# Larger modulation runs, 96-row latent attention, and an issue order planned by other TensorE prices

## The chip, the cores and the metric

The kernel runs on one core of one Trainium2 chip. The metric is the device time of one execution in microseconds (us). A core has a matrix engine (TensorE, PE in the rows; its weight loads are PEld), a vector engine (DVE), a scalar engine (ACT), GpSimd (POOL), and a queue (SP) that issues the DMA transfers.

## The reference

Two networks one after the other, on 256 tokens of width 1024 and, in the first, 256 context tokens. Cut to what matters here:

```python
# first block, two layers: nine modulation vectors of 1024 for the tokens and nine for the context
mod_x = (jax.nn.silu(c) @ w_ada[l] + b_ada[l])[:, None, :]        # w_ada[l]: 1024 x 9216
mod_c = jax.nn.silu(c_ctx) @ w_ada[l] + b_ada[l]
h = h + 0.5 * g1 * _swiglu(_modulate(_rms_norm(h, norm_ffn1[l]), sh1, sc1), ...)
# then attention with windows, global and neighbourhood, and a second feed-forward net

# second block, one layer: a recurrent mixer in chunks (rwkv), latent attention (mla),
# differential attention, a gated merge, a feed-forward net with a convolution
q = (_rmsnorm(c_q, q_norm) @ w_uq).reshape(B, S, 8, 64 + 32)       # latent attention, 8 heads
q_rope = _apply_rope(q[..., 64:], cos, sin)                       # a part of 32 for each head
kv = (_rmsnorm(c_kv, kv_norm) @ w_ukv).reshape(B, S, 8, 64 + 64)
k_rope = _apply_rope(k_rope, cos, sin)                            # one part of 32 for all heads
logits = einsum(q_nope, k_nope) + einsum(q_rope, k_rope)          # over 64 and over 32
probs = _masked_softmax(logits * scale, mask)                     # causal
```

## The kernel before

The program is written once without an order: `Plan` records every operation with its engine, its operands and a cost from `Plan.cost`, and `Plan.schedule` then plays the engines forward in time. Whenever an engine is free in that play it takes the first ready operation in the order of writing whose buffers can be had. `emit` writes the instructions out in the order found, so each engine's order is fixed when the kernel is built. All come from one line of `emit` (L739 in the rows). Buffers are pages of SBUF (`page`), a small area (`small`), three slots for weights (`w`) and eight PSUM banks (`bank`).

Dense products split every f32 number into two f32r parts and take three f32r matmuls for each block (`mm3`). Other products stay in f32, and each of those stands as two passes in the trace.

The modulation vectors are made by `ada_steps`: for each layer five groups of up to 2048 columns, each in eight steps over the 1024 inputs. A step loads 1 MB of `w_ada` and issues four matmuls (two in the last group) that each use 32 columns of the array, so the four stand side by side. The steps are the filling (`fill`): one is popped after each block of a feed-forward net, which is where the planner then places its matmuls among the dense ones, one by one. The first group of the first layer runs in the setup.

Latent attention (`mla_diff`) keeps the 64-row parts of q and k in `qn` and `kn` (two heads in a tile, on 64 rows each) and the 32-row parts in `qr` and `kr` (on 32 rows each). The scores of one head and query tile are one matmul over 64 rows and one over 32 rows, added up in PSUM. A block of matmuls that uses part of the array has that shape as its "tile": the rows show it as rows*columns, 128*128 being the whole array.

`Run` puts several TensorE operations into one that the planner doesn't split.

Of the kernel before, what the change touches and what calls it, by code (L numbers as in the profile page):

```python
# [18 lines left out]
P = 128  # L19
# [368 lines left out]
class Plan:  # L388
# [20 lines left out]
    def record(self, eng, method, a, k):  # L409
        if self.open_run is not None:  # L410
            assert eng == "tensor"
            self.open_run.append((method, a, k))
            return None
        if method == "run":
            reads, writes, cost = [], [], 0.0
            for m_, a_, k_ in a:
                r_, w_ = self.operands(a_, k_)
                cost += self.cost(eng, m_, a_, k_, r_, w_)[0]
                reads += r_
                writes += w_  # L420
            return self.note(eng, method, a, {}, reads, writes, k["cost"] or cost, None)
# [50 lines left out]
    def cost(self, eng, method, a, k, reads, writes):  # L472
# [8 lines left out]
        src_ps = any(r.buf.kind == "ps" for r in reads)  # L481
        if eng == "tensor":
            if method == "transpose":
                return 110, None
            f32r = any(s[0] == "d" for s in reads[0].chain) or reads[0].buf.dt == F32R
            n = sh[1]
            for d in sh[2:]:
                n *= d
            if f32r and sh[0] == 32:
                return 75, None  # L490
            if f32r:
                return max(107, n / 2.4) + 1, None
            if sh[0] == 32 or o.index()[1] and sh[0] <= 64:
                return (0.52 * n if sh[0] == 32 else max(60, n / 0.95)), None
            return (max(109, n / 0.6) if sh[0] > 64 else max(107, n / 0.6)), None
        ns = [int(np.prod(r.shape[1:])) for r in reads]
# [17 lines left out]
    def schedule(self, n_pages, n_small, n_w, window, margin, n_banks=8):  # L514
# [44 lines left out]
        front, dma_free, t, n_done = 0, 0.0, 0.0, 0  # L559
        table, used = None, -1e9  # L560
        done = [False] * N
# [90 lines left out]
        while n_done < N:  # L652
            for e in engs:
                if busy[e] > t:
                    continue
                h, skipped, pick = ready[e], [], None
                while h and len(skipped) < 48:
                    i = heapq.heappop(h)
                    tab = ops[i][7]
                    if e == "scalar" and tab and tab != table and t - ready_at[i] < TABLE_WAIT and t - used < TABLE_WAIT:  # L660
                        heapq.heappush(events, (t + 300.0, 2, -1))
                        skipped.append(i)
                    elif can(i):
                        pick = i
                        break
                    else:
                        skipped.append(i)
                for i in skipped:
                    heapq.heappush(h, i)
                if pick is None:  # L670
                    continue
                cost, tab, lat = ops[pick][6:9]
                if e == "scalar" and tab:
                    if tab != table:
                        cost += 1283
                        table = tab
                    used = t + cost
# [63 lines left out]

TABLE_WAIT = 2500.0


class Build:
# [134 lines left out]
    def ada_steps(self, l, g):  # L880

        nc = self.nc
        n = min(2048, 9 * D - 2048 * g)
        nj = n // 512
        st = {}

        early = l == 0 and g == 0

        def load(k):
            def f():  # L890
                if k == 0:
                    st["ps"] = self.aux_ps("ada")
                raw = self.sb.tile([P, 2048], F32, name="araw", tag="araw0" if early else "araw",
                                   bufs=8 if early else 3)
                nc.sync.dma_start(raw[:, :n], self.a["w_ada"][l, k, :, 2048 * g:2048 * g + n])
                for j in range(nj):
                    nc.tensor.matmul(st["ps"][32 * j:32 * j + 32, :], self.cs[:, k, :],
                                     raw[:, 512 * j:512 * j + 512], start=(k == 0), stop=(k == KB - 1),
                                     skip_group_check=True, tile_position=(0, 32 * j))
            return f  # L900

        def fin():
            np_ = 32 * nj
            t = self.t("adat", [512])
            nc.vector.tensor_copy(t[:np_], st["ps"][:np_])
            pt = self.aux_ps("adaT")
            for b in range(4):
                nc.tensor.matmul(pt[:, 8 * b:8 * b + 8], t[:np_, 128 * b:128 * b + 128], self.rsel[:np_],
                                 start=True, stop=True)
            view = pt[:, :32].rearrange("p (b j r) -> p b j r", b=4, j=4)[:, :, :nj]  # L910
# [3 lines left out]
            for m in range(2 * g, 2 * g + nj // 2):  # L914
# [6 lines left out]
                elif m in (2, 8):  # L921
                    nc.vector.tensor_scalar(self.hg[l][m // 8], w, 0.5, None, op0=OP.mult)
        return [load(k) for k in range(KB)] + [fin]

# [950 lines left out]

    def rope32(self, dst, src):
# [6 lines left out]
        nc.vector.tensor_tensor(dst, t1, t2, op=OP.add)  # L1883

    def mla_diff(self, u):
# [31 lines left out]
        for i in range(3):  # L1917
# [5 lines left out]
            cn.append(c)  # L1923
        kr, qr = self.s2("kr", (S,)), self.s2("qr")
        self.rope32(kr, x[3])
        qn, kn = ([self.s2(f"{n}{i}") for i in range(2)] for n in ("qn", "kn"))
        w = self.wtile(a["w2_uq"])
        for i in range(3):
# [3 lines left out]
            if i < 2:  # L1932
                nc.scalar.copy(qn[i].rearrange("p a b -> p (a b)"), ps)
            else:
                t = self.t512("qrt")
                nc.scalar.copy(t, ps)
                for j in range(2):
                    self.rope32(qr[:, j], t[:, S * j:S * j + S])
        w = self.wtile(a["w2_ukv"])
        for i in range(2):  # L1940
            ps = self.mm_ps("pkn")
            for j in range(2):
                self.dense(ps[:, S * j:S * j + S], w, (2 * i + j) * P, cn[2:], nk=1)
            nc.scalar.copy(kn[i].rearrange("p a b -> p (a b)"), ps)
        vm = [self.s2(f"vm{i}", (512,)) for i in range(2)]
# [24 lines left out]
        def transposed(pr):  # L1970
            pt = self.aux_ps("PT2")
            for i in range(3):
                nc.tensor.transpose(pt[:, P * i:P * i + P], pr[:, P * i:P * i + P], self.ident)
            pts = self.t512("pts")
# [3 lines left out]
        for b in range(4):  # L1978
            yp = self.aux_ps("y")
            for s in range(2):  # L1980
                h = 2 * b + s
                hs = slice(64 * s, 64 * s + 64)
                rr = slice(32 * (h % 4), 32 * (h % 4) + 32)
                ps = self.aux_ps("Sml")
                for qt, (c0, c1) in enumerate(span):
                    qs = slice(P * qt, P * qt + P)
                    N = c1 - c0
                    nc.tensor.matmul(ps[:, c0:c1], qn[b // 2][hs, b % 2, qs], kn[b // 2][hs, b % 2, :N],
                                     start=True, stop=False)
                    nc.tensor.matmul(ps[:, c0:c1], qr[rr, h // 4, qs], kr[rr, :N], start=False, stop=True,  # L1990
                                     tile_position=(32 * (h % 4), 0))
                d = diag(ps[:, :3 * P])
# [4 lines left out]
                for i, (c0, c1) in enumerate(span):  # L1997
                    nc.vector.tensor_scalar(pr[:, c0:c1], pr[:, c0:c1], st[:, 4 + i:5 + i], None, op0=OP.mult)
                pts = transposed(pr)
                for qt in range(2):  # L2000
                    for kb in range(qt + 1):
                        c0 = (qt + kb) * P
                        nc.tensor.matmul(yp[hs, P * qt:P * qt + P], vm[kb][:, 64 * h:64 * h + 64], pts[:, c0:c0 + P],
                                         start=(kb == 0), stop=(kb == qt), skip_group_check=True)
            o = self.s2(f"oml{b}", (2, S), F32R)
# [78 lines left out]
def build(tc, aps, out):  # L2084
# [5 lines left out]
    b.second()  # L2090
    order = plan.schedule(N_PAGES, N_SMALL, W_SLOTS, 3000, dict(m=4096, s=64))
    with tc.tile_pool(name="sb", bufs=1) as sb, tc.tile_pool(name="ps", bufs=1, space=PSUM) as ps, tc.manual_schedule():
# [26 lines left out]
```

## Time and profile before

| | |
|---|---|
| median of 3 runs | 2465.49 us (2462.23 to 2465.62) |
| the profiled execution | 2465.52 us, of which the span of the trace is 2463.7 us |
| TensorE busy | 2419.1 us (98%), 14630 matmuls |
| VectorE, ScalarE, GpSimd busy | 1342.4 us (54%), 971.2 us (39%), 46.5 us (2%) |
| DMA | 133 GB/s on the mean |

The ends of matmuls are modelled in such a profile, and consecutive ones overlap, so 98% says that the matrix engine always has one in its pipe and not that it is at its peak. What one matmul costs is read from how many start in a stretch of known length. A row that counts matmuls in a stretch also counts the one to three whose tail reaches over its edges.

### The profile page before, as it was taken

What the parts mean: (1) busy time and instruction counts of PE and PEld (TensorE: products, weight loads), DVE (VectorE), ACT (ScalarE), POOL (GpSimd) and SP (SyncE); (2) the same over time, 40 slices, a digit from 0 to 9 for tenths busy, and PEclk for the clock granted to TensorE, in tenths of its full rate; (3) what the DMA queues carried; (4) which work ended last, traced back from release to release, by engine and by line L of the source; (5) the groups of instructions that cost most, each with busy time, mean ns of one, the idle gap of its engine ahead of it and who ended that gap; (6) DMA issues with size and microseconds to landing.
All of it is one profiled execution on the core that took longest, in us unless ns stands there. A gap on an engine that the chain in (4) does not pass through costs nothing. (4 is left out here: it accounts for less than half of the span.)

```text
span 2463.7 us, 35734 instructions
## 1 busy us (share of the span) xinstructions
PE 2419.1 (98%) x14630; PEld 2036.2 (83%) x14630; DVE 1342.4 (54%) x2533; ACT 971.2 (39%) x1748; POOL 46.5 (2%) x62
## 2 busy tenths in 40 slices
PE   7999999999999999999999999999999999999998
PEld 5777776978787677778878889889999897999998
DVE  4323332585753389335323347866567665657874
ACT  3222222476642122223212235755456122556653
POOL 0000000000000000000000000000000000000000
PEclk8999999999999999999999999999999997999999
DMA  7526523212234454343224223135554011354543
GB/s 312 205 103 240 197 87 127 95 44 87 85 137 161 146 190 180 131 156 139 91 71 137 75 100 103 61 113 178 196 171 164 22 52 35 104 190 169 190 168 123
DMA packets 55043, 328.35 MB, mean 133 GB/s; under 512 B 7134, under 2 KB 10206, under 8 KB 24799
## 3 DMA queue, kind: packets, MB, share of 16 engines
q1 hardware_dynamic: 54878, 326.07, 37.1%
q8 instruction: 114, 1.87, 0.3%
q14 instruction: 51, 0.41, 0.1%
HBM read 325.00 MB, written 1.05 MB: 132 GB/s over the span
## 5 line engine op out<-in xcount | busy, mean ns | idle before, releaser
L739 PE MATMUL bank<-page,page 128*128 128x256 f32 (+8 forms) x13152 | 2296.3, 346 | 29.0 <-DMA page<-in_w_ada_dram 13.2
L739 PEld LDWEIGHTS bank<-page,page 128*128 128x128 f32 (+3 forms) x13152 | 1876.1, 186 | 373.8 <-issue 95.1
L739 ACT CAST page<-w 128x1024 fp32r<-128x1024 f32 (+2 forms) x511 | 489.1, 961 | 1067.6 <-PE bank L739 1027.6
L739 DVE TENSOR_TENSOR page<-w,page 128x1024 fp32r<-128x1024 f32 (+2 forms) x511 | 567.8, 1113 | 591.5 <-ACT page L739 457.8
L739 DVE TENSOR_TENSOR page<-page,bank 128x512 f32<-128x512 f32 (+2 forms) x170 | 94.2, 570 | 245.3 <-PE bank L739 244.1
L739 PE MATMUL bank<-page 128*128 128x256 f32 (+5 forms) x650 | 167.0, 325 | 1.9 <-DVE page L739 1.3
L739 DVE SCALAR_TENSOR_TENSOR page<-bank,small,page 128x256 f32<-128x256 f32 (+2 forms) x240 | 111.5, 484 | 103.8 <-PE bank L739 100.2
L739 DVE TENSOR_TENSOR page<-page,page 128x256 fp32r<-128x256 f32 (+3 forms) x271 | 128.6, 490 | 12.1 <-ACT page L739 11.5
L739 ACT ACTIVATE page<-bank,small 128x256 f32<-128x256 f32 (+2 forms) x216 | 115.1, 546 | 37.3 <-DVE small L739 24.8
L739 PEld LDWEIGHTS bank<-page 128*128 128x128 f32 (+2 forms) x650 | 109.8, 188 | 15.9 <-issue 4.2
L739 ACT CAST page<-page 128x256 fp32r<-128x256 f32 (+1 forms) x167 | 78.2, 481 | 97.0 <-DVE page L739 86.5
L739 ACT COPY page<-bank 128x512 f32<-128x512 f32 (+2 forms) x163 | 77.6, 511 | 96.5 <-PE bank L739 91.1
L739 PEld LDWEIGHTS bank<-small,page 128*128 128x128 f32 (+1 forms) x760 | 93.2, 167 | 25.0 <-issue 8.7
L739 PE MATMUL bank<-small,page 128*128 128x128 f32 (+4 forms) x760 | 108.8, 269 | 4.1 <-ACT page L739 2.8
L739 ACT ACTIVATE page<-bank 128x512 f32<-128x512 f32 (+3 forms) x168 | 84.2, 508 | 61.3 <-PE bank L739 57.8
L739 ACT ACTIVATE page<-page 128x256 f32<-128x256 f32 (+3 forms) x180 | 78.0, 446 | 67.0 <-DVE page L739 60.0
L739 DVE TENSOR_TENSOR page<-bank,page 128x256 f32<-128x256 f32 (+2 forms) x123 | 57.5, 489 | 55.4 <-PE bank L739 29.6
L739 DVE TENSOR_REDUCE small<-bank 128x1 f32<-128x512 f32 (+3 forms) x132 | 67.5, 527 | 4.3 <-PE bank L739 4.0
L739 POOL TENSOR_TENSOR small<-small 128x2 f32<-128x2 f32 (+2 forms) x32 | 34.4, 1078 | 1874.3 <-DVE small L739 1382.8
L739 ACT ACTIVATE page<-page,small 128x256 fp32r<-128x256 f32 (+1 forms) x124 | 56.7, 507 | 30.5 <-DVE page L739 30.0
L739 DVE COPY_PREDICATED page<-page,small 128x384 f32<-128x384 uint32 x124 | 64.9, 590 | 1.0
L739 DVE TENSOR_SCALAR page<-page,small 128x256 f32<-128x256 f32 (+2 forms) x136 | 53.6, 408 | 2.2 <-ACT page L739 1.1
(46 smaller groups left out, 383.2 us busy)
## 6 DMA issues: line engine op xcount, KB each, us to landing
w<-in_gu_dram SPq DMA_DIRECT2D x88, 1024.0 KB, 5.0
page<-in_w_ada_dram SPq DMA_DIRECT2D x64, 1024.0 KB, 4.9
w<-in_dn_dram SPq DMA_DIRECT2D x64, 704.0 KB, 4.1
w<-in_w_up_dram SPq DMA_DIRECT2D x22, 1024.0 KB, 4.8
w<-in_w_qk_dram SPq DMA_DIRECT2D x12, 1024.0 KB, 4.8
w<-in_w_gate_dram SPq DMA_DIRECT2D x12, 1024.0 KB, 4.9
w<-in_w_dn_dram SPq DMA_DIRECT2D x16, 704.0 KB, 4.0
page<-in_w_ada_dram SPq DMA_DIRECT2D x16, 512.0 KB, 3.5
```

Source lines behind the costliest of these rows:

```text
L739: getattr(getattr(self.real, eng), m_)(*a_, **k_)
```

## The change

It has five parts. (1) In all groups of the modulation but the first, a step loads two pieces and issues their matmuls as one run that isn't split; in the last group of each layer (two matmuls for a piece) the two pieces go to different columns of the array. The loads have four buffers in place of three. (2) Latent attention copies both parts of q and k into tiles of 96 rows (`qh`, `kh`), with one matmul per head and query tile; ScalarE copies heads of 64 rows, VectorE writes the turned 32 rows head by head, GpSimd copies the shared `kr` to four heads at once, twice. (3) The two heads of a pair then share one run for the product with v. (4) `Plan.cost` has other prices for matmuls and gives each the shape that it uses, and `Plan.schedule` charges 100 ns for another shape and lets TensorE take a ready operation of the same shape ahead of one of another for up to 1.5 us. (5) The margin that stays free in SBUF when an operation is taken out of turn is 6144 in place of 4096.

```diff
             if method == "transpose":
-                return 110, None
-            f32r = any(s[0] == "d" for s in reads[0].chain) or reads[0].buf.dt == F32R
...
-            if f32r:
-                return max(107, n / 2.4) + 1, None
...
+                return 109, (128, 128, True)
+            mode = tuple(32 if x <= 32 else 64 if x <= 64 else 128 for x in (rows, cols)) + (False,)
+            if any(s[0] == "d" for s in reads[0].chain) or reads[0].buf.dt == F32R:
+                return max(107, n / 2.4) + 13.3, mode
+            return max(223 if mode[1] == 128 else 109, n / 0.6 + 8), mode
...
+                    if e == "tensor" and tab != shape and other is None and t - ready_at[i] < SHAPE_WAIT:
+
+                        other = i
+                        continue
...
+                if e == "tensor" and tab != shape:
+                    cost += 100
+                    shape = tab
...
-                for j in range(nj):
-                    nc.tensor.matmul(st["ps"][32 * j:32 * j + 32, :], self.cs[:, k, :],
...
+                with nc.run(cost=nk * nj * 215.0 + 200.0):
+                    for i, raw in enumerate(raws):
+                        k = k0 + i
+                        for j in range(nj):
+                            c = 32 * (j if nj == 4 else j + nj * i)
+                            nc.tensor.matmul(st["ps"][c:c + 32, :], self.cs[:, k, :], raw[:, 512 * j:512 * j + 512],
...
+        qh, kh = ([self.s2(f"{n}{i}", (4, S)) for i in range(2)] for n in ("qh", "kh"))
+        for i in range(2):
+            nc.gpsimd.tensor_copy(kh[i][64:96], kr[64:96, None, :].to_broadcast([32, 4, S]))
...
-                    nc.tensor.matmul(ps[:, c0:c1], qn[b // 2][hs, b % 2, qs], kn[b // 2][hs, b % 2, :N],
-                                     start=True, stop=False)
-                    nc.tensor.matmul(ps[:, c0:c1], qr[rr, h // 4, qs], kr[rr, :N], start=False, stop=True,
-                                     tile_position=(32 * (h % 4), 0))
+                    nc.tensor.matmul(ps[:, c0:c1], qh[h // 4][:96, h % 4, P * qt:P * qt + P],
+                                     kh[h // 4][:96, h % 4, :c1 - c0], start=True, stop=True)
...
+            with nc.run(cost=3 * 215.0):
                 for qt in range(2):
                     for kb in range(qt + 1):
...
-    order = plan.schedule(N_PAGES, N_SMALL, W_SLOTS, 3000, dict(m=4096, s=64))
+    order = plan.schedule(N_PAGES, N_SMALL, W_SLOTS, 3000, dict(m=6144, s=64))
```

Where the instructions stand now is read from the orders of the two programs. On TensorE, in the first layer's first feed-forward net, the modulation's matmuls (output 32x512, from `page_75`, which holds the silu of c) stood one at a time between the dense ones of a down projection:

```order
L739 MATMUL bank_70<-page_768,page_192 128x512
L739 MATMUL bank_71<-page_2122,page_75 32x512
L739 MATMUL bank_70<-page_199 128x512 x2
L739 MATMUL bank_70<-page_199,page_192 128x512
L739 MATMUL bank_70<-page_2014,page_199 128x512 x2
L739 MATMUL bank_70<-page_2014,page_192 128x512
L739 MATMUL bank_70<-page_2075,page_199 128x512 x2
L739 MATMUL bank_70<-page_2075,page_192 128x512
L739 MATMUL bank_70<-page_204,page_199 128x512 x2
L739 MATMUL bank_70<-page_204,page_192 128x512
L739 MATMUL bank_71<-page_2122,page_75 32x512
```

In the changed program eight of them stand together, four from each of two loads, again within a down projection:

```order
L747 MATMUL bank_68<-page_864,page_534 128x512 x2
L747 MATMUL bank_68<-page_864,page_225 128x512
L747 MATMUL bank_72<-page_396,page_239 128x512 x2
L747 MATMUL bank_74<-page_78,page_75 32x512 x4
L747 MATMUL bank_74<-page_961,page_75 32x512 x4
L747 MATMUL bank_72<-page_396,page_534 128x512
L747 MATMUL bank_72<-page_396,page_239 128x512 x2
```

Over the whole program the 288 modulation matmuls stood in 97 such groups: 3 of the setup, 32 of one matmul, 58 of two to four, 4 of five or six. Now they stand in 39: the same 3 of the setup, 28 of eight and 8 of four. Changes of shape on TensorE (transposes counted as a shape of their own) fell from 517 to 326.

On TensorE in the second block, the scores of latent attention: `page_10404` holds `qn` or `kn` (64 rows), `page_1431` `qr` (32 rows), the banks are the score tiles; a `small` input is the unit matrix of a transpose.

```order
L739 MATMUL bank_72<-page_10404,page_75 128x128
L739 MATMUL bank_72<-page_1431,page_13336 128x128
L739 MATMUL bank_72<-page_10404,page_75 128x256
L739 MATMUL bank_72<-page_1431,page_13336 128x256
L739 MATMUL bank_74<-page_10404,page_75 128x128
L739 MATMUL bank_74<-page_1431,page_13336 128x128
L739 MATMUL bank_74<-page_10404,page_75 128x256
L739 MATMUL bank_74<-page_1431,page_13336 128x256
L739 MATMUL bank_73<-small,page_3990 128x128
L739 MATMUL bank_70<-page_10404,page_13336 128x128
L739 MATMUL bank_73<-small,page_3990 128x128 x2
L739 MATMUL bank_70<-page_1431,page_13336 128x128
```

In the changed program `page_75` and `page_13377` are `kh`, `page_3927` and `page_4081` `qh`; `bank_73` takes a dense product.

```order
L747 MATMUL bank_73<-page_1873,page_5322 128x512
L747 MATMUL bank_70<-page_75,page_3927 128x128
L747 MATMUL bank_70<-page_75,page_3927 128x256
L747 MATMUL bank_67<-page_75,page_3927 128x128
L747 MATMUL bank_67<-page_75,page_3927 128x256
L747 MATMUL bank_69<-small,page_9752 128x128
L747 MATMUL bank_72<-small,page_9752 128x128
L747 MATMUL bank_71<-page_75,page_3927 128x128
L747 MATMUL bank_68<-page_75,page_3927 128x128
L747 MATMUL bank_68<-page_75,page_3927 128x256
L747 MATMUL bank_71<-page_75,page_3927 128x256
L747 MATMUL bank_73<-page_198,page_84 128x256
```

Thirty-two score matmuls over part of the rows became sixteen over the whole array, with dense ones between the heads. GpSimd, which ran five TENSOR_TENSOR in a row here, now has the two copies among them:

```order
L747 TENSOR_TENSOR small<-small 128x8
L747 TENSOR_TENSOR small<-small 128x4 x2
L747 COPY page_75<-page_9752 32x1024
L747 COPY page_13377<-page_9752 32x1024
L747 TENSOR_TENSOR small<-small 128x4
```

The first score matmul waits for the first copy, the fifth head's for the second; the 128x4 behind them belongs to the recurrent mixer's norm.

## Rows read from the trace of the kernel before

**Rows 1.** The page: span, engines, and TensorE's granted clock in 40 slices.
```profile
span 2463.7 us, 35734 instructions
PE 2419.1 (98%) x14630; PEld 2036.2 (83%) x14630; DVE 1342.4 (54%) x2533; ACT 971.2 (39%) x1748; POOL 46.5 (2%) x62
PEclk8999999999999999999999999999999997999999
```

**Rows 2.** The chain that ended last: start, length, engine, count of instructions.
```profile
1677.24 191.94 PE bank L739 x1599
2020.61 115.13 PE bank L739 x688
```

**Rows 3.** Whom TensorE waited for: us in total, times, longest.
```profile
PE bank L739 <- DMA page<-in_w_ada_dram: 13.2, 5, 6.6
PE bank L739 <- ACT page L739: 11.3, 19, 1.8
PE bank L739 <- DVE page L739: 10.0, 16, 2.3
PE bank L739 <- POOL small L739: 2.3, 5, 1.1
```

**Rows 4.** TensorE in chosen stretches: dense, six groups, eight singles, one and two ranks.
```profile
core 0: us, PE busy (x), PEclk, DMA share, GB/s
1320.00:1476.00 156.00, 156.00 (x690) 1.00 0.27 91
258.31:330.95 72.64, 72.64 (x339) 1.00 0.41 152
396.14:435.71 39.57, 39.57 (x150) 1.00 0.26 93
330.95:331.94 0.99, 0.99 (x10) 1.00 0.00 0
64.91:66.75 1.84, 1.84 (x14) 1.00 0.01 4
```

**Rows 5.** The latent scores' stretch: TensorE and its clock before and after 2062 us.
```profile
2055.18:2062.00 6.82, 6.82 (x42) 1.00 0.43 143
2062.00:2093.22 31.22, 31.22 (x81) 0.50 0.01 4
```

**Rows 6.** TensorE by shape, 2055.18 to 2093.22 us.
```profile
L739 PE MATMUL bank<-page,page 32*128 32x256 f32 x16 | 9.2, 673 | 0.0
L739 PE MATMUL bank<-page,page 64*128 64x256 f32 x16 | 8.7, 641 | 0.0
L739 PE MATMUL bank<-page,page 64*128 64x128 f32 x16 | 5.7, 454 | 0.0
L739 PE MATMUL bank<-page,page 32*128 32x128 f32 x16 | 5.7, 452 | 0.0
```

**Rows 7.** TensorE: 24 f32 passes of 128 columns, and 4 of 256.
```profile
2007.34:2009.93 2.59, 2.59 (x26) 1.00 0.27 111
1560.52:1561.39 0.87, 0.87 (x6) 1.00 0.88 367
```

**Rows 8.** All engines (PE, PEld, DVE, ACT, POOL) in the scores' stretch and behind it.
```profile
2055.18:2093.22 38.04, 38.04 (x121) 22.40 (x120) 15.24 (x54) 9.63 (x33) 1.05 (x1) 0.59 0.08 29
2093.22:2130.00 36.78, 36.78 (x266) 34.20 (x266) 14.88 (x30) 15.75 (x29) 0.00 (x0) 0.96 0.32 110
```

**Rows 9.** Groups on GpSimd, ScalarE and VectorE that are nearest to the added copies.
```profile
L739 POOL MEMSET page<- 64x512 f32 x20 | 10.4, 520 | 449.2 <-PE bank L739 448.5
L739 ACT COPY page<-bank 128x256 f32<-128x256 f32 x50 | 16.8, 376 | 15.3 <-PE bank L739 14.9
L739 DVE TENSOR_TENSOR page<-page,bank 64x256 f32<-64x256 f32 x6 | 2.5, 422 | 2.7 <-PE bank L739 2.0 <-ACT page L739 0.6
```

**Rows 10.** All engines, 20 to 40 us; then the transfers of w_ada.
```profile
20.00:40.00 20.00, 11.79 (x61) 6.93 (x62) 11.90 (x29) 8.52 (x18) 0.00 (x0) 0.69 1.02 415
page<-in_w_ada_dram SPq DMA_DIRECT2D x64, 1024.0 KB, 4.9
```

More of the change, by code (lines that the diff above doesn't have):

```diff
@@ L417, in record @@
                 r_, w_ = self.operands(a_, k_)
-                cost += self.cost(eng, m_, a_, k_, r_, w_)[0]
+                c_, mode = self.cost(eng, m_, a_, k_, r_, w_)
+                cost += c_
                 reads += r_
                 writes += w_
-            return self.note(eng, method, a, {}, reads, writes, k["cost"] or cost, None)
+            return self.note(eng, method, a, {}, reads, writes, k["cost"] or cost, mode)
         reads, writes = self.operands(a, k)
@@ L482, in cost @@
         if eng == "tensor":
+            n = int(np.prod(sh[1:]))
+            rows, cols = reads[0].shape[0], int(np.prod(reads[0].shape[1:]))
             if method == "transpose":
-                return 110, None
-            f32r = any(s[0] == "d" for s in reads[0].chain) or reads[0].buf.dt == F32R
[L486 to L490, printed above, removed]
-            if f32r:
-                return max(107, n / 2.4) + 1, None
-            if sh[0] == 32 or o.index()[1] and sh[0] <= 64:
-                return (0.52 * n if sh[0] == 32 else max(60, n / 0.95)), None
-            return (max(109, n / 0.6) if sh[0] > 64 else max(107, n / 0.6)), None
+                return 109, (128, 128, True)
[3 more added lines that the diff above has]
+            return max(223 if mode[1] == 128 else 109, n / 0.6 + 8), mode
         ns = [int(np.prod(r.shape[1:])) for r in reads]
@@ L559, in schedule @@
         front, dma_free, t, n_done = 0, 0.0, 0.0, 0
-        table, used = None, -1e9
+        table, used, shape = None, -1e9, None
         done = [False] * N
@@ L655, in schedule @@
                     continue
-                h, skipped, pick = ready[e], [], None
+                h, skipped, pick, other = ready[e], [], None, None
                 while h and len(skipped) < 48:
@@ L667, in schedule @@
                         skipped.append(i)
+                if other is not None:
+                    if pick is None and can(other):
+                        pick = other
+                    else:
+                        skipped.append(other)
                 for i in skipped:
@@ L742 @@
 TABLE_WAIT = 2500.0
+SHAPE_WAIT = 1500.0
 class Build:
@@ L887, in ada_steps, with load @@
         early = l == 0 and g == 0
-        def load(k):
+        nk = 1 if early else 2
+        def load(k0):
             def f():
-                if k == 0:
+                if k0 == 0:
                     st["ps"] = self.aux_ps("ada")
-                raw = self.sb.tile([P, 2048], F32, name="araw", tag="araw0" if early else "araw",
-                                   bufs=8 if early else 3)
-                nc.sync.dma_start(raw[:, :n], self.a["w_ada"][l, k, :, 2048 * g:2048 * g + n])
-                for j in range(nj):
-                    nc.tensor.matmul(st["ps"][32 * j:32 * j + 32, :], self.cs[:, k, :],
-                                     raw[:, 512 * j:512 * j + 512], start=(k == 0), stop=(k == KB - 1),
-                                     skip_group_check=True, tile_position=(0, 32 * j))
+                raws = []
+                for k in range(k0, k0 + nk):
+                    raw = self.sb.tile([P, 2048], F32, name="araw", tag="araw0" if early else "araw",
+                                       bufs=8 if early else 4)
+                    nc.sync.dma_start(raw[:, :n], self.a["w_ada"][l, k, :, 2048 * g:2048 * g + n])
+                    raws.append(raw)
+                with nc.run(cost=nk * nj * 215.0 + 200.0):
[4 more added lines that the diff above has]
+                            nc.tensor.matmul(st["ps"][c:c + 32, :], self.cs[:, k, :], raw[:, 512 * j:512 * j + 512],
+                                             start=k < (1 if nj == 4 else 2), stop=k >= KB - (1 if nj == 4 else 2),
+                                             skip_group_check=True, tile_position=(0, c))
@@ L900, in load @@
             return f
         def fin():
-            np_ = 32 * nj
             t = self.t("adat", [512])
-            nc.vector.tensor_copy(t[:np_], st["ps"][:np_])
+            nc.vector.tensor_copy(t, st["ps"])
             pt = self.aux_ps("adaT")
+            m = 2 * nj
             for b in range(4):
-                nc.tensor.matmul(pt[:, 8 * b:8 * b + 8], t[:np_, 128 * b:128 * b + 128], self.rsel[:np_],
-                                 start=True, stop=True)
+                for c in range(0, 8, m):
+                    nc.tensor.matmul(pt[:, 8 * b:8 * b + m], t[:, 128 * b:128 * b + 128], self.rsel[:, c:c + m],
+                                     start=c == 0, stop=c + m == 8)
@@ L922, in fin @@
                     nc.vector.tensor_scalar(self.hg[l][m // 8], w, 0.5, None, op0=OP.mult)
-        return [load(k) for k in range(KB)] + [fin]
+        return [load(k) for k in range(0, KB, nk)] + [fin]
     def norm_add(self, r, k, scale=1.0, key=None):
@@ L1874, in conv_ffn, with rope32 @@
             nc.sync.dma_start(self.out[:, k], t)
-    def rope32(self, dst, src):
+    def rope32(self, dsts, src):
         nc = self.nc
@@ L1882, in rope32 @@
         nc.vector.tensor_tensor(t2, pr[:, :S], self.rope2[:, 1], op=OP.mult)
-        nc.vector.tensor_tensor(dst, t1, t2, op=OP.add)
+        for dst, rows in dsts:
+            nc.vector.tensor_tensor(dst, t1[rows], t2[rows], op=OP.add)
     def mla_diff(self, u):
@@ L1923, in mla_diff, with heads @@
             cn.append(c)
-        kr, qr = self.s2("kr", (S,)), self.s2("qr")
-        self.rope32(kr, x[3])
-        qn, kn = ([self.s2(f"{n}{i}") for i in range(2)] for n in ("qn", "kn"))
+        kr = self.s2("kr", (S,))
+        self.rope32([(kr, slice(0, P))], x[3])
+        qh, kh = ([self.s2(f"{n}{i}", (4, S)) for i in range(2)] for n in ("qh", "kh"))
+        for i in range(2):
+            nc.gpsimd.tensor_copy(kh[i][64:96], kr[64:96, None, :].to_broadcast([32, 4, S]))
+        def heads(dst, i, ps):
+            for j in range(2):
+                for s in range(2):
+                    nc.scalar.copy(dst[i][:64, 2 * j + s], ps[64 * s:64 * s + 64, S * j:S * j + S])
         w = self.wtile(a["w2_uq"])
@@ L1932, in mla_diff @@
             if i < 2:
-                nc.scalar.copy(qn[i].rearrange("p a b -> p (a b)"), ps)
+                heads(qh, i, ps)
             else:
@@ L1937, in mla_diff @@
                 for j in range(2):
-                    self.rope32(qr[:, j], t[:, S * j:S * j + S])
+                    self.rope32([(qh[j][64:96, h], slice(32 * h, 32 * h + 32)) for h in range(4)],
+                                t[:, S * j:S * j + S])
         w = self.wtile(a["w2_ukv"])
@@ L1943, in mla_diff @@
                 self.dense(ps[:, S * j:S * j + S], w, (2 * i + j) * P, cn[2:], nk=1)
-            nc.scalar.copy(kn[i].rearrange("p a b -> p (a b)"), ps)
+            heads(kh, i, ps)
         vm = [self.s2(f"vm{i}", (512,)) for i in range(2)]
@@ L1971, in transposed @@
             pt = self.aux_ps("PT2")
-            for i in range(3):
-                nc.tensor.transpose(pt[:, P * i:P * i + P], pr[:, P * i:P * i + P], self.ident)
+            with nc.run():
+                for i in range(3):
+                    nc.tensor.transpose(pt[:, P * i:P * i + P], pr[:, P * i:P * i + P], self.ident)
             pts = self.t512("pts")
@@ L1979, in mla_diff @@
             yp = self.aux_ps("y")
+            ptss = []
             for s in range(2):
                 h = 2 * b + s
-                hs = slice(64 * s, 64 * s + 64)
-                rr = slice(32 * (h % 4), 32 * (h % 4) + 32)
                 ps = self.aux_ps("Sml")
                 for qt, (c0, c1) in enumerate(span):
-                    qs = slice(P * qt, P * qt + P)
-                    N = c1 - c0
-                    nc.tensor.matmul(ps[:, c0:c1], qn[b // 2][hs, b % 2, qs], kn[b // 2][hs, b % 2, :N],
-                                     start=True, stop=False)
-                    nc.tensor.matmul(ps[:, c0:c1], qr[rr, h // 4, qs], kr[rr, :N], start=False, stop=True,
-                                     tile_position=(32 * (h % 4), 0))
+                    nc.tensor.matmul(ps[:, c0:c1], qh[h // 4][:96, h % 4, P * qt:P * qt + P],
+                                     kh[h // 4][:96, h % 4, :c1 - c0], start=True, stop=True)
                 d = diag(ps[:, :3 * P])
@@ L1998, in mla_diff @@
                     nc.vector.tensor_scalar(pr[:, c0:c1], pr[:, c0:c1], st[:, 4 + i:5 + i], None, op0=OP.mult)
-                pts = transposed(pr)
+                ptss.append(transposed(pr))
+            with nc.run(cost=3 * 215.0):
                 for qt in range(2):
@@ L2002, in mla_diff @@
                         c0 = (qt + kb) * P
-                        nc.tensor.matmul(yp[hs, P * qt:P * qt + P], vm[kb][:, 64 * h:64 * h + 64], pts[:, c0:c0 + P],
-                                         start=(kb == 0), stop=(kb == qt), skip_group_check=True)
+                        for s in range(2):
+                            h, hs = 2 * b + s, slice(64 * s, 64 * s + 64)
+                            nc.tensor.matmul(yp[hs, P * qt:P * qt + P], vm[kb][:, 64 * h:64 * h + 64],
+                                             ptss[s][:, c0:c0 + P], start=(kb == 0), stop=(kb == qt),
+                                             skip_group_check=True)
             o = self.s2(f"oml{b}", (2, S), F32R)
```

## The prediction

> **What bounds the kernel now.** I read the page first: TensorE has something in its pipe in 2419.1 of the span's 2463.7 us, at the full clock but for a few slices [rows 1]. The reader is to see that no other engine comes near. The chain that ended last says the same by place: its long pieces are TensorE alone, among them 1677 to 1869 us and 2020.61 to 2135.74 us, the second across all of latent attention [rows 2]. The table of waits completes it: TensorE waited 36.8 us in all for others, 13.2 of them for modulation weights, nearly all in the setup [rows 3]. So time is saved where TensorE's own stream gets shorter, and lost where a new order makes it wait. I then priced pieces of this stream in stretches of known content, not by the busy time of a group, whose ends are modelled and overlap.
>
> **Modulation runs.** A stretch of dense 512-column f32r matmuls alone holds 690 in 156.00 us, two of them tails over the edges, so one costs 156.00/688 = 0.2267 us [rows 4]. The stretch 258.31 to 330.95 us runs from the start of one modulation group to that of the sixth after it; between two stands one gate-and-up block of 48 dense matmuls. 72.64 less 288 x 0.2267 (65.29) leaves 7.35 us for six groups: 1.22 us for a group of four matmuls side by side. In 396.14 to 435.71 us eight groups of a single matmul stand among 4 x 33 = 132 dense ones: 39.57 less 29.92 leaves 9.65, or 1.21 us each. So one matmul costs what four cost: the price is that of one rank (two passes of 512 columns) and of the way into the 32-column shape and back. A second rank in the same group costs less, since the way is paid once: a group of six matmuls, two ranks, lasted 1.84 us from its first start to the next dense one, a group of one rank 0.99 us. Two ranks together cost 1.22 + 0.85 = 2.07 us.
>
> The setup's three groups stay. Of the other 94, by the order, 32 hold one matmul (38.7 us), 58 two to four (70.8) and 4 five or six (8.3): 117.8 us. The change has 28 groups of eight, two ranks (58.0 us), and 8 of four on four strips (9.8): 67.8 us. **Saved: 50.0 us.** The prices are good to about 0.02 us a group, so 48 to 52. It moves no weight bytes away; it asks for two loads together. In a gate-and-up step, 48 x 0.2267 + 2.07 = 12.95 us, three loads of 1.05 MB make 243 GB/s; in a down step, 33 x 0.2267 + 2.07 = 9.55 us, 2.82 MB make 295 GB/s. The queue moved 415 GB/s from 20 to 40 us [rows 10], so I take no wait for it; the cover is the block before, and the case without it is a rival below. The last group of each layer needs 8 small products more: 2 x 8 x 2 passes x 0.108 [rows 7] = 3.5 us, less the 64-row shapes that they no longer use. I take +1 (0 to 3.5).
>
> **Latent scores.** From the first score to the last, 2055.18 to 2093.22 us, TensorE took 38.04 us [rows 5]. 64 of its 121 passes are scores, sixteen of each kind [rows 6]; two are tails, 55 belong to the recurrent mixer, the transposes and the products with v. The change makes the scores sixteen matmuls over the whole array: sixteen passes of 128 columns at 2.59/24 = 0.108 us and sixteen of 256 at 0.87/4 = 0.218 [rows 7], 1.7 + 3.5 = 5.2 us. No trace shows 96 rows; a row count below 128 on the whole array I price as 128, since the columns set the two prices. The other 55 passes cost 55 x 0.108 = 5.9 us at least; with their shapes of 64 columns I take 7. That makes 12.2 us. **Saved: 25.8 us.** The upper bound is 26.9 (5.9 for the rest).
>
> The lower bound hangs on the clock. It was granted at 1.00 up to 2062 us and at 0.50 (1.2 of 2.4 GHz) from there past the end of the scores, although TensorE is shown busy all of that time: 31.22 of 31.22 us [rows 5]. What it did before the fall was the end of the recurrent mixer and the first 32- and 64-row scores. I take it that with the part-of-the-array shapes gone the clock stays up; if it falls all the same, 12.2 becomes 24.4 us and the gain 13.6. The Trainium skill (TensorE: Matmul & The Clock Gate, Part 1) says that the half clock is the default and that a busy engine is released from it. By that rule a stretch shown fully busy would not have fallen to 0.50, so the trace does not agree with it as the busy time is modelled here. If the rule is taken at its word, something other than the shapes lowered the clock, it may do so again, and the sum would be 12.2 us higher; that is the first rival.
>
> What this edit adds: twelve more copies on ScalarE (sixteen of 64x256 for four of 128x512), at most 0.376 us each; six more adds on VectorE at 0.422 (rows of the nearest shapes, [rows 9]); two GpSimd copies of 1024 elements, which no row shows. The nearest is a memset of 512 elements in 520 ns, so 1.0 us at its rate and 4.2 at four times that; I take 2. The cover: from 2055 to 2130 us, 74.8 us, VectorE was busy 30.1 and ScalarE 25.4 [rows 8]. Pressed into 49 us they have 32.7 and 29.9 to do: still below TensorE, but no longer far below. Ahead of the first score, which waits for GpSimd, some ninety matmuls stand after the product that `kr` is made from, over 10 us, so the two copies and three VectorE operations fit; if that cover went, the first score would be late by up to 4 us, once. The 128x4 operation queued behind the copies serves the mixer's norm, whose result is used only in the merge. The shared run for v makes the first head wait for the second; dense products stand in between. I take all of it at nothing.
>
> **The new order.** The 1.5 us of preference for the same shape moves many other instructions a little; of the 191 shape changes saved, 116 are the modulation's and the rest stand at the scores and at transposes. The price of a 256-column f32r matmul in the plan goes from 108 to 120 ns. TensorE was thus some 10% slower on the chip than in the old plan, which gave every other engine and each transfer some slack; the new plan has less of it, and the larger margin lets fewer operations run ahead. The bounds are the waits that exist: a gain of 12 us (half of the 23.6 outside the modulation rows goes) and a loss of as much as exists now, 24. I take +2.
>
> **The sum**, against the profiled execution (2465.52 us, of which 1.8 outside the span; the median of the runs is 2465.49, the same): 2465.5 - 50.0 - 25.8 + 1 + 2 = 2392.7, so 2393 us.
>
> **Rivals.** *The clock falls anyway.* For it: the half clock began among work that stays, in part, as it was. Against it: 64 of the passes there, most of the time, go. It gives 2393 + 12 = 2405 us. *The exact plan costs waits.* With its slack gone, TensorE waits for VectorE or ScalarE in the attention stages, or for filling that the margin holds back. For it: those engines supply nearly all of its waits today [rows 3], and the score stage gets denser. Against it: in 2020 to 2135 us the chain didn't pass over them once [rows 2]. With 12 to 35 us it gives 2405 to 2428. *The waits shrink too:* what is planned by true prices fits better; with 15 to 25 us less than taken, 2368 to 2378. *Slower than before:* the paired loads. A run waits for the later of its two, and each weight tile queued behind them on SP comes 1 MB later. If a run stands on TensorE before its loads have landed, everything dense behind it stands too. It decides from 72.8/36 = 2.0 us of waiting per run; a full time to landing, 4.9 us [rows 10], for all 36 would give 2393 + 176 = 2569. Against it: the rates above, and planned steps of 10 us and more. *The change doesn't do it:* the order excludes that for groups and scores, but new waits can eat all of it (2461 to 2470), needing over twice the waits of today.
>
> **How the numbers follow.** The forecast as summed (2380 to 2402) has 60 in 100, the clock 13, waits 12, fewer waits 10, no change 2, the paired loads 3. The predicted time is the first case's. The range takes in the clock's case, the larger part of the waits' and half of the better one's: 2374 to 2416. About 0.2% (5 us) is what a measurement of this kernel can tell from no change; by the cases it is faster with 0.95, the same with 0.02, slower with 0.03.
>
> **What would show it.** Right: 36 groups of the 32-column shape behind the setup, with steps of 12.95 us from group to group in the gate-and-up blocks; no rows of 32 in TensorE's shapes; a stretch of scores in which dense matmuls fill and the clock stays at 1.00; TensorE's waits for DMA still near 13 us. Wrong: a first score that waits for GpSimd by microseconds; a clock of 0.50 there again; a table of waits in which VectorE or ScalarE has grown by tens of us; modulation waits outside the setup. The prediction is wrong most easily by the waits, which no row of before prices.

## The result and the profile after

The changed kernel takes 2408.34 us (median of 4 runs, 2404.77 to 2412.12) against 2465.55 before: ratio 0.9771, 95% interval 0.9753 to 0.979. That is 57.2 us saved where 72.8 were forecast, inside the range of 2374 to 2416 and above the likeliest case's own 2380 to 2402. Its four executions were granted 0.987 to 0.991 of TensorE's full clock, and the time goes with that (2412.12 us at 0.987, 2404.77 at 0.991), so which stretches stand at half clock below is told for one execution only. The page of the profiled execution (2410.36 us), for [rows 1]:

```profile
span 2408.6 us, 35710 instructions
PE 2356.2 (98%) x14614; PEld 2033.1 (84%) x14614; DVE 1340.8 (56%) x2539; ACT 971.1 (40%) x1760; POOL 47.5 (2%) x64
PEclk8999999999999999999999999999999999999999
```

TensorE is still the bound, and the slice with the "7" has gone. Its stretches, for [rows 4, 5]: a gate-and-up step and a down step with a run of two ranks, a step with one rank, the scores, then three pieces ahead of them and the second block, which the experiments use as their yardstick (TensorE's columns only):

```profile
core 0: us, PE busy (x), PEclk, DMA share, GB/s
81.00:94.00 13.00, 13.00 (x66) 1.00 0.61 242
200.18:209.78 9.60, 9.60 (x50) 1.00 0.74 288
928.32:940.43 12.11, 12.11 (x58) 1.00 0.46 173
2030.41:2039.84 9.43, 8.98 (x60) 1.00 0.00 1
1863.60:1867.00 3.40, 3.40 (x16) 0.50 0.40 166
1897.70:1901.10 3.40, 3.37 (x16) 0.50 0.73 236
2010.40:2020.60 10.20, 9.56 (x43) 0.50 0.00 0
1821.10:2141.80 320.70, 310.20 (x2349) 0.97 0.25 86
```

The steps were forecast as 12.95 and 9.55 us. The scores run at the full clock. But three pieces ahead of them, 17.0 us together, run at 0.50. The reader can see what came before the longest in TensorE's timeline (start, length; in brackets how long it had waited, and for whom):

```profile
2005.76 1.57 PE L747 MATMUL bank<-page,page 128*128 128x256 f32 x10
2008.82 0.49 PE L747 MATMUL bank<-small 128*128 128x128 f32 x2 [1.48 <-POOL small L747]
2009.14 1.82 PE L747 MATMUL bank<-page,page 128*128 128x64 f32 x16
2011.58 0.69 PE L747 MATMUL bank<-small,page 128*128 128x128 f32 x2 [0.62 <-DVE page L747]
```

The waits of the whole program, for [rows 3]:

```profile
PE bank L747 <- ACT page L747: 14.3, 24, 1.7
PE bank L747 <- DMA page<-in_w_ada_dram: 13.5, 5, 6.7
PE bank L747 <- DVE page L747: 11.5, 22, 1.3
PE bank L747 <- POOL small L747: 5.2, 5, 1.5
```

They sum to 44.5 us where they were 36.8, and those for DMA are all in the setup. Before, the chain that ended last was TensorE alone across all of latent attention, 2020.61 to 2135.74 us [rows 2]. Now it has these pieces between 1990 and 2060 us (the longest):

```profile
1989.90 15.46 PE bank L747 x127
2007.36 1.37 DVE page L747 x3
2014.61 10.30 PE bank L747 x57
2024.94 0.36 ACT page L747
2027.57 1.67 DVE page L747 x5
2039.07 2.40 ACT page L747 x8
2043.15 2.25 ACT page L747 x8
2046.52 13.54 PE bank L747 x124
```

From 2024.94 to 2046.52 us it passes over ScalarE and VectorE without touching TensorE. All engines in that stretch (PE, PEld, DVE, ACT, POOL), for [rows 8]; below it the new copies on GpSimd and VectorE's eight adds over 32 rows, which the edit put in place of two over 128 rows:

```profile
2024.94:2046.52 21.58, 20.59 (x144) 17.77 (x142) 20.47 (x72) 17.58 (x51) 1.05 (x1) 1.00 0.15 50
```

```profile
L747 POOL COPY page<-page 32x1024 f32<-32x1024 f32 x2 | 2.4, 1238 | 0.1
L747 DVE TENSOR_TENSOR page<-page,page 32x256 f32<-32x256 f32 x8 | 3.3, 418 | 0.2
```

Seven of these eight adds, 0.42 us each between 2029.26 and 2036.42 us, are links of that chain.

### The profile page after: what moved, and what is told of

It is laid out like the page before. It is cut to its first block, busy times and chain, and to the rows that moved or that the text cites. A ratio compares the mean times of both kernels' runs of the same rounds, so it can differ in the third digit from the quotient of the medians.

```text
span 2408.6 us, 35710 instructions
## 1 busy us (share of the span) xinstructions
PE 2356.2 (98%) x14614; PEld 2033.1 (84%) x14614; DVE 1340.8 (56%) x2539; ACT 971.1 (40%) x1760; POOL 47.5 (2%) x64
## 4 chain that ended last, share of the span: by engine, by line
PE 66%; issue 24%; DVE 6%; ACT 2%; DMA 1%; POOL 1%; SPq 0%; POOLq 0%; DVEq 0%; ACTq 0%
PE bank L747 66%; DVE page L747 4%; ACT page L747 2%; DVE small L747 1%; DMA page<-in_w_ada_dram 1%; POOL small L747 1%; DVE bank L747 0%; ACT L747 0%; SPq L747 0%; POOL page L747 0%; POOLq L2147 0%; ACT small L747 0%; DVEq L2147 0%; DVEq L747 0%; POOLq L747 0%
## 5 line engine op out<-in xcount | busy, mean ns | idle before, releaser
L747 PE MATMUL bank<-page,page 128*128 128x256 f32 (+5 forms) x13309 | 2244.9, 344 | 31.5 <-DMA page<-in_w_ada_dram 13.5
L747 PEld LDWEIGHTS bank<-page,page 128*128 128x128 f32 (+2 forms) x13309 | 1886.5, 186 | 324.7 <-issue 62.9
L747 DVE TENSOR_TENSOR page<-page,page 128x256 fp32r<-128x256 f32 (+3 forms) x283 | 133.7, 489 | 18.3 <-ACT page L747 16.9
L747 PE MATMUL bank<-page 128*128 128x256 f32 (+5 forms) x461 | 116.6, 321 | 2.3 <-ACT page L747 1.3
L747 PEld LDWEIGHTS bank<-small,page 128*128 128x128 f32 x776 | 97.4, 170 | 25.0 <-DVE page L747 7.0
L747 ACT COPY page<-bank 128x512 f32<-128x512 f32 (+3 forms) x175 | 80.6, 499 | 85.8 <-PE bank L747 77.7
L747 PEld LDWEIGHTS bank<-page 128*128 128x128 f32 (+2 forms) x461 | 75.9, 188 | 11.0 <-DVE page L747 3.0
```

Of the source, the lines that this page charges most:

```text
L747: getattr(getattr(self.real, eng), m_)(*a_, **k_)
```

## The experiments

**Theory A:** the two edits bring what their terms say, and the new order costs some 14 us instead of 2. **Theory B:** the edits themselves fall short, and the order is neutral. One yardstick for all: the second block between 80.0 and 87.5% of the dense f32r columns, the same work in every version (recurrent mixer, latent and differential attention). It took 334.8 us before:

```profile
1860.80:2195.60 334.80, 329.75 (x2382) 0.94 0.24 83
```

**E1, the modulation runs alone**, with their margin:

```diff
+        nk = 1 if early else 2
+                with nc.run(cost=nk * nj * 215.0 + 200.0):
...
+    order = plan.schedule(N_PAGES, N_SMALL, W_SLOTS, 3000, dict(m=6144, s=64))
```

> The kernel before with the modulation runs alone (two ranks in one run, four load buffers, the margin of 6144 that goes with them), old prices, no shape preference. Theory A, the forecast's prices hold and the new order is what costs: 2465.5 - 48 = 2416 to 2420 us. Theory B, the runs themselves fall short, by waits for paired loads or by a dearer second rank: 2424 to 2432. TensorE's waits for DMA stay near 13 us by A and grow by several us by B.

2418.92 us, 47.1 less than before (ratio 0.9809, 0.9796 to 0.9822); TensorE waits 13.4 us for DMA. The second block, and the piece of it at half clock:

```profile
1815.20:2150.00 334.80, 329.64 (x2381) 0.94 0.24 83
2013.70:2051.20 37.50, 37.50 (x104) 0.50 0.05 19
```

**E2, the 96-row tiles alone** (with the shared product with v, and the three transposes of a head in one run, which belongs to the change as well):

```diff
+                    nc.tensor.matmul(ps[:, c0:c1], qh[h // 4][:96, h % 4, P * qt:P * qt + P],
+                                     kh[h // 4][:96, h % 4, :c1 - c0], start=True, stop=True)
```

> The kernel before with the 96-row tiles and the shared product with v alone, old planner. Theory A: the stage pays what the trace after shows or more, 2465.5 - 22 to - 26 = 2439 to 2444 us; the clock may still fall for some 10 us behind the recurrent mixer, as in the trace after. Theory B, the missing us lie in this edit, in a first score that waits or in copies that VectorE and ScalarE have no time for: 2448 to 2456.

2437.72 us, 28.3 less (0.9887, 0.9872 to 0.9901), a little better than either theory. The second block, and the scores from the first to the next product:

```profile
1862.70:2168.00 305.30, 298.89 (x2350) 1.00 0.26 91
2055.32:2064.91 9.59, 8.70 (x59) 1.00 0.01 3
```

29.5 us are gone from the block, and no half clock is left in it. E1 keeps it with the old scores, E2 loses it with the new ones.

**E3, the planner alone:**

```diff
+SHAPE_WAIT = 1500.0
...
+                if e == "tensor" and tab != shape:
+                    cost += 100
+                    shape = tab
```

> The kernel before with the planner's part alone: prices, shapes, 1.5 us of preference, margin. Theory A, the new order costs: it is slower than before although it saves some changes of shape, 2468 to 2480 us, with more waits for ScalarE, VectorE and GpSimd and a longer half clock in the setup. Theory B, the order is neutral: 2461 to 2467. A third reading, the new order gains and hides a larger shortfall of the two edits: under 2460.

2457.21 us, 8.8 less (0.9966, 0.9954 to 0.9978): under 2460, as in the third reading. Changes of shape fall from 517 to 429. The second block takes 323.6 us; its half clock is down to one piece, which begins with a wait of TensorE for VectorE:

```profile
2072.30:2082.50 10.20, 8.91 (x41) 0.50 0.00 0
```

```profile
2073.59 2.18 PE L747 MATMUL bank<-small,page 128*128 128x128 f32 x9 [1.40 <-DVE page L747]
```

So the order alone gets part of what E2 gets, on the same old scores. From the first of them to the last the shape changes 24 times instead of 41; that this is the reason isn't shown. Elsewhere it loses: TensorE waits 20.8 us for modulation weights instead of 13.2.

**E4, both edits, old order:** E1 and E2 together.

> Both edits (modulation runs and 96-row tiles) with the old prices and no shape preference; only the margin is the new one. Theory A, the order alone is what the forecast sized wrong: 2465.5 - 48 - 24 = 2390 to 2397 us, faster than the changed kernel by 11 to 18. Theory B, the edits fall short by themselves: 2405 to 2411, as the changed kernel. Third reading, the order gains: over 2413.

2394.47 us (0.9702, 0.9687 to 0.9716), 71.6 less than before: theory A. The new prices and the preference cost 2408.3 - 2394.5 = 13.9 us behind the edits; the margin of 6144 is in both kernels. The second block takes 12.5 us less than in the changed kernel:

```profile
1817.30:2125.50 308.20, 301.79 (x2349) 0.99 0.26 90
```

**E5 and E6: preference or prices?**

```diff
-SHAPE_WAIT = 1500.0
+SHAPE_WAIT = 0.0
```

> The changed kernel without the preference for the same shape (0 in place of 1.5 us); new prices, the charge of 100 ns and the margin stay. If holding back an urgent operation of another shape is what costs the 14 us that both edits lose with the new order: 2392 to 2398 us, waits and half clock as with the old order. If the prices cost it, by leaving the plan no slack: 2405 to 2411. Between these: both have a part.

2411.12 us (0.9774, 0.9761 to 0.9788): the prices (the charge of 100 ns is one of them), not the preference. The counterpart:

```diff
-                return max(107, n / 2.4) + 13.3, mode
+                return max(107, n / 2.4) + 1, mode
...
-                    cost += 100
-    order = plan.schedule(N_PAGES, N_SMALL, W_SLOTS, 3000, dict(m=6144, s=64))
+    order = plan.schedule(N_PAGES, N_SMALL, W_SLOTS, 3000, dict(m=7168, s=64))
```

(and the old f32 prices).

> Both edits with the preference of 1.5 us, but the old prices and no charge for a change of shape (margin 7168, as with 6144 no plan is found). The counterpart of the run without preference: if the preference costs, 2404 to 2412 us; if the prices cost, 2392 to 2398.

2389.87 us (0.9685, 0.9672 to 0.9699), the fastest version found, 18.5 below the changed kernel. Its second block, and its chain from 1995 to 2045 us:

```profile
1817.70:2118.70 301.00, 297.52 (x2349) 1.00 0.27 92
```

```profile
1994.94 50.09 PE bank L751 x404
```

The chain is TensorE alone again, and VectorE and ScalarE have the same work as in the changed kernel. The waits there:

```profile
PE bank L751 <- ACT page L751: 1.7, 2, 1.1
PE bank L751 <- DVE page L751: 1.5, 5, 0.4
```

**E7, four ranks in a run** (old order):

```diff
-        nk = 1 if early else 2
+        nk = 1 if early else 4 if nj == 4 else 2
...
-                                       bufs=8 if early else 4)
+                                       bufs=8 if early else 6)
```

> Both edits with the old order, but four ranks in a run instead of two in the eight full groups behind the setup (14 runs of sixteen matmuls and two of eight in place of 28 of eight), six load buffers. If only the way into the 32-column shape is paid once and a further rank costs 0.85 us: 14 ways of 0.37 us less than with two ranks, - 5 us, 2389 to 2391. If four loads of 1 MB together make a run wait, or six buffers take room that the planner needs: 2396 to 2410.

2397.15 us (0.9713, 0.97 to 0.9727), no gain. The price itself fell: a gate-and-up step of 14.67 us less 48 x 0.2267 is 3.79 us for four ranks, against 2 x 2.12. But one run stood on TensorE before its loads had landed:

```profile
823.45 1.07 PE L739 MATMUL bank<-page,page 128*32 128x512 f32 x8 [1.32 <-DMA page<-in_w_ada_dram]
825.93 1.07 PE L739 MATMUL bank<-page,page 128*32 128x512 f32 x8 [1.42 <-DMA page<-in_w_ada_dram]
828.43 1.93 PE L739 MATMUL bank<-page,page 128*32 128x512 f32 x8 [1.43 <-DMA page<-in_w_ada_dram]
834.33 2.07 PE L739 MATMUL bank<-page,page 128*128 128x512 f32 x4 [3.96 <-DVE page L739]
```

This is the forecast's rival of the paired loads, at four ranks: three waits for DMA, one for VectorE, and the clock at 0.50 from 828.30 to 838.50 us.

**E8, the margin alone** (6144 in the kernel before):

> The kernel before with the margin of 6144 alone. The margin was changed in the runs with the modulation edit as well; if it costs nothing, 2463 to 2468 us; if fewer operations that run ahead cost waits, 2469 to 2476.

2460.17 us (0.9974, 0.9962 to 0.9985), 6.1 less, outside both expectations. A margin that does no work moves a plan by 6 us, and E1's 47.1, E3's 8.8 and E4's 71.6 may each hold some of that.

**E9 to E11: which price, and is it slack?** E9 puts back the dense price (the first line of E6's diff), E10 the f32 prices without the charge; E11 keeps all new prices and delays what TensorE takes from others, in the plan alone:

```diff
-                    heapq.heappush(events, (end + lat[ops[u][0]], 3, u))
+                    late = 400.0 if ops[u][0] == "tensor" != e else 0.0
+                    heapq.heappush(events, (end + lat[ops[u][0]] + late, 3, u))
```

> The changed kernel with one price put back: a dense f32r matmul of 256 columns is planned at 108 ns, as before, and not at 120; f32 prices, the charge, the preference and the margin stay. If the exact price of the dense matmuls, which fill between the small stages, is what takes the plan's slack: 2388 to 2396 us, with waits and half clock in the second block as in the run with all old prices. If the f32 prices or the charge do it: 2405 to 2411.

> The counterpart: the old prices for f32 matmuls and no charge for a change of shape, the new price of 120 ns for a dense f32r matmul of 256 columns. If the dense price takes the slack: 2403 to 2411 us. If the f32 prices or the charge do: 2388 to 2396.

> The changed kernel with all its new prices, but the plan lets TensorE take a result of another engine or a transfer only 400 ns after it is planned to be there. If lost slack is the mechanism, and not a wrong price, the waits go back to what they are with the old prices: 2386 to 2396 us. If the new prices mislead in another way (which operation goes first): 2403 to 2411. If late starts cost more than they save: over 2411.

2399.01 us (0.9729, 0.9715 to 0.9742), 2392.77 (0.97, 0.9687 to 0.9713) and 2401.65 (0.974, 0.9727 to 0.9753). E9 and E11 fell between their cases. Against the changed kernel the old dense price alone brings 9.3 us (E9), the old f32 prices without the charge 15.6 (E10), the slack 6.7 (E11); so the f32 prices or the charge cost most.

**E12, the changed kernel with a margin of 7168:**

> The changed kernel with a margin of 7168 in place of 6144, all new prices and the preference kept. It is the counterpart of the run with old prices and preference, which needed this margin, and it tells how far a plan's time is scattered by a change that means nothing. If the new prices cost by rule: 2403 to 2413 us. If the margin gave that run its gain, or if the plan with 6144 was merely an unlucky one: 2386 to 2397.

2410.47 us (0.9772, 0.9759 to 0.9786): not the margin, and not one unlucky plan. The second block in these versions, one execution of each, from its windows and waits (the half clock from the clock's record):

| | second block, us | TensorE waits in it | of it at half clock |
|---|---|---|---|
| changed kernel | 320.7 | 10.0 | 17.0 |
| E5, no preference | 317.5 | 10.0 | 17.0 |
| E12, margin 7168 | 317.6 | 10.1 | 10.2 |
| E4, old order | 308.2 | 6.0 | 6.8 |
| E9, old dense price | 309.1 | 6.7 | 3.4 |
| E10, old f32 prices | 308.1 | 5.6 | 6.8 |
| E11, 400 ns of slack | 306.3 | 7.0 | 3.4 |
| E6, old prices and preference | 301.0 | 3.2 | 0 |

All three plans with the full new prices and no slack stand at 317.5 us and more, all others at 309.1 and less. E11 shows that slack alone, with the new prices kept, brings the stage back; of the 14.4 us gained there it gives 6.8 away elsewhere (its span is 2401.0 us against 2408.6), among it some 4 us in the first layer, around and behind its attention (470 to 740 us).

## Why the prediction was right, and what it missed

**Modulation runs: right.** A run of two ranks costs 13.00 - 48 x 0.2267 = 2.12 us (2.07 forecast), one rank 12.11 - 10.88 = 1.23 (1.22). 28 x 2.12 + 8 x 1.23 = 69.2 us: 48.6 saved for 50.0, and 47.1 on the chip in E1, margin included. The paired loads cost nothing: 242 and 288 GB/s in the steps, all waits for DMA in the setup. The median landing time of a 1 MB load of modulation weights grew from 4.9 to 6.6 us and stayed covered. The Trainium skill (TensorEngine Tiling, Key Properties) says that another tiling mode drains TensorE. The rows agree in that a change costs time: two runs cost 4.24 us, the same matmuls in one run 3.79 (E7), so one way in and out takes 0.45 us here. That this time is a drain no row shows.

**Latent scores: right, slightly too small.** 28.3 us in E2 for the 25.8 forecast. The stretch of scores took 9.59 us there for 12.2, but its 59 passes hold 26 others beside the 32 scores and a tail, where the forecast had 55, so the two lengths can't be compared. The score passes themselves came as priced: 16 x 0.112 + 16 x 0.217 = 5.3 us for 5.2. How much of the 28.3 us is the clock's was not separated. GpSimd's copy takes 1.24 us (2 taken, 1.0 to 4.2 bounded), and no first score waited for it. The eight adds were taken at nothing too; with the old order none of them is on the chain (E2, E4), in the changed kernel seven are. "With the part-of-the-array shapes gone the clock stays up" holds in E2. The rule that the prediction weighs, that a busy engine is released from the half clock (the Trainium skill, TensorE: Matmul & The Clock Gate, Part 1), still has a stretch against it: TensorE is shown busy 37.50 of 37.50 us in E1, at 0.50. E3 says that the shapes are not the whole of it, since the same scores with fewer changes had 10.2 us of it, and these began with a wait.

**The new order: the step that failed.** "I take +2" was 13.9 (E4 against the changed kernel). With the two edits at 71.6 for 74.8, this term is 11.9 of the 15.6 us that the forecast missed. One caveat: the prediction's term includes the margin, and E4's 71.6 has the margin in it. If the 6.1 us of E8 carry over to E4, the edits brought 65.5 and the whole new order cost 7.8; no run has both edits with the old margin. What came is the forecast's own rival of the exact plan, priced at 2405 to 2428 and given 12 in 100. So the time lies in the range because the range took in the rivals. The two profiled executions lie 15.9 us apart (2410.36 and 2394.47 us). Of these, 12.5 lie in the second block: 4.0 in longer waits and, at half of 10.2 us more of half clock, about 5; the other 3.4 are in TensorE's busy time (310.20 us against 301.79) and were not traced. The setup adds 3, with 3.4 us more of half clock in it (20.5 us, 17.1 in E4). The step also failed in a sentence that looked safe: "still below TensorE, but no longer far below". In 21.58 us VectorE was busy 20.47, and the chain of the changed kernel runs over it and ScalarE from 2024.94 to 2046.52 us. E6 shows that the order decides: from 2005.00 to 2026.50 us its VectorE was busy 20.33 of 21.50 us, and its chain is TensorE's.

**The clock's rival** came in part: the scores ran at full clock, but three pieces ahead of them did not. Each of the three begins within 2 us of a wait of TensorE (0.5 to 1.5 us), and E6, with 3.2 us of waits there, has none. That the waits lowered the clock is not shown, though. In E10 it fell at 1932.20 us with no wait in the 7 us before, and TensorE shown busy throughout:

```profile
1925.00:1932.20 7.20, 7.20 (x60) 1.00 0.13 18
1932.20:1939.00 6.80, 6.80 (x27) 0.50 0.33 136
```

**What stays open.** The f32 prices and the charge were not taken apart, and E9 and E10 overlap: either put back is enough for the second block. That lost slack is the mechanism is shown there (E11, and E5 and E12 as the plans without it) and not for the setup, nor for the first layer, where slack cost. Why the preference gains 4.6 us under the old prices (E4 to E6) was not separated from E6's margin; under the new prices that margin brought nothing (E12).

## What to carry to other kernels

A planner's wrong prices can be its slack: when they are made exact, give the slack back on purpose. Here that paid where the engines were densest, and cost elsewhere. Price a change of order by a run of its own: edits that are summed from rows were right to 3 us of 75 (with the margin's share among them), the order around them was off by 12. Change what should do nothing, such as a margin, in a run of its own too: here it moved the time by 6 us. When a stage is pressed, compare the busy time of its second engine with the new length; at 20.47 of 21.58 us the order decided here whether it was on the chain.

## What the runs showed of the hardware

A wait of TensorE can cost more than its length: 1.48 us for GpSimd was followed by 10.20 us at 0.50, in which TensorE was busy 9.56. In E7 a run that takes 3.57 us on the median took 13.26 to the next dense matmul: 4.2 us are waits for DMA, 4.0 the wait for VectorE at its end, and 1.6 are left for the half clock. Other waits as long were not followed by a fall: the same wait for GpSimd, 1.48 us to 2047.83 us in E3, stands at full clock before and after, as does one of 1.08 us in E4's mixer. What decides was not settled. A pass over 96 rows takes about what one over 128 does (0.108 and 0.218 us) [rows 7]: in the changed kernel 0.112 us for 128 columns and 0.217 for 256, from start to start.
